# Decoder step on one core: decode masks on another engine, two margins, score order, and reordered first and last steps

## The chip, the cores and the metric

The kernel runs on one core of a Trainium2 chip. The metric is the device time of one execution in microseconds. Engines are named as in the profile: PE is TensorE's matrix multiply and PEld its weight loads, DVE is VectorE, ACT is ScalarE, POOL is GpSimd, SP is SyncE. DMAs are issued from queues on SP, ACT and POOL.

## The reference

One layer of a decoder handles 256 prompt tokens and 8 x 4 decode tokens (288 columns in all), width 2048. It takes an RMS norm and one input projection, then three groups: a short gated convolution (512 channels), sparse attention with 8 query heads in 2 key groups (a compressed, a selected and a window branch), and cross-attention to 256 memory tokens. Each is gated, the three are concatenated, and one output projection, a residual add and a last RMS norm follow.

```python
h = rms_norm(x, norm_g)
c_h, c_b, c_c, c_g, q, n_g, b_g, kv6, m_q, m_g = split_cols(h @ w_in)
...
imp = jnp.where(forced[None, :, None, :], FORCE, imp)
_, idx = lax.top_k(imp, top)                  # 16 blocks of 64 cached keys
s2 = jnp.einsum('bgthd,bgtkjd->bgthkj', qrg, kg) * ATTN_SCALE
p2 = masked_softmax(s2, smask, axis=(-2, -1))
...
return x + mixed @ w_out, kv_new, win_state, conv_new
```

For the decode tokens the selected branch runs over 2048 cached keys per request. The kernel computes the scores of all 2048 and masks the blocks that are not among the chosen ones. The norm needs a reciprocal square root of a mean of squares per token.

## The kernel before

All large products are split in float32r: an operand is taken as a high and a low half (`wh`, `wl` for weights), and three of the four partial products are summed. A weight half tile is 128 x 1024. It is loaded by DMA (`w_load`, from SP at first and from POOL later, five buffers), copied to its high half by ACT (`w_hi`), and the low half is the difference, taken by DVE (`w_lo`). A half tile of the input projection gives 24 matmuls (`product_half`, `run_half`). Everything else is fitted between them.

The order of the work is written by a planner inside the program, at build time. `chunk()` is called after every 12 matmuls and lets each live generator (`spawn`) run to its next `yield`. A list `at` estimates how far PE, the loads, DVE (`VEC`), ACT and SP have come. `until(engine, margin)` yields at least one chunk and goes on only when PE's estimate has passed that engine's estimate plus the margin. The default margin `WAIT` is 0.8; `AHEAD`, -1.5, lets an instruction be placed early. DVE and ACT work issued through `vec` and `act` moves the estimates; work issued straight to POOL (`nc.gpsimd`) does not. Each engine carries out its instructions in the order in which they were written, and waits where data is missing.

What the change touches:

- `first_tiles` (helper of the start): the first two column tiles of the memory projection in float32, from k-tiles that DVE scales as they land (`m_scale`, four k-tiles a call, with a copy of the high half on ACT). `m_low` takes the low half on DVE, `first_loads` issues loads on SP. `part(i, k, n)` issues n k-tiles of column tile i. In the trace these products are `zf`.
- `rsqrt`: called in `token_rstd` (the memory tokens), in `sum_x` (the input tokens) and in `factors` (three times, at the end). One Newton step after it corrects the first value.
- `scores`: scores of four groups of cached keys (512 columns) against the decode queries, in PSUM (`sk`), copied by ACT into a stretch of the wide tile `S`. There is one `S` for each half of the batch (`hf` 0 and 1).
- `dec_cmp`, `dec_softmax`: the compressed branch's importances give `madd`, which is 0 for a chosen block and -1e30 for another. `dec_softmax` adds it to the four stretches of selected scores, takes maxima, exponentials and the scaling, and transposes. It ends by setting a flag that the value products (`winv_use`, `selv_use`, in the trace `od`) wait for.
- `weights`: transposes 512 columns of `S` in four pieces (`pv` in the trace) before each value product.
- `prompt_cmp`, `prompt_nsa`: the prompt's attention. Their transposes are `pct` and `pt`.
- The end: the last 512 output columns come as rows (`zr`), the decode rows from `decode_rows` (`zd`, 16 k-steps of four column groups). `squares`, `factors`, `spread_rows` (`rb`), `scale_rows` and `scale_tiles` do the last norm, each followed by its output DMA. `spread_rows(1, ...)` stands among the decode rows after `SPREAD_AT` k-steps. `busy` fills PE with products that nobody reads.

The decode output is split for the second output pass by `split_decode`; the second pass starts when that has been written.

Of the kernel before, what the change touches and what calls it, by code (L numbers as in the profile page):

```python
# [71 lines left out]
WARM = 3  # L72
LOW_FIRST = 22
TAIL_BUSY = (4, 6)
SPREAD_AT = 13
DT = 12
ROWS = 512

# [2 lines left out]
def decode_step(ctx, tc, xT, xN, xD, xL, fgl, memT, cst, w_in, w_mem, w_out, w_bg, pt, ptv, ckc, ckk, ckv, wk, wv, mk, mv,  # L81
# [112 lines left out]
    def C(name):  # L194
        o, w = _COFF[name]
        return c[:, o:o + w]
# [3 lines left out]
    def rsqrt(r, ssq, rest=None, room=None):  # L200

        v, t = room or (small(3, "yv", 1)[:, :r.shape[1]], small(3, "yt", 1)[:, :r.shape[1]])
        if rest is not None:
            act.activation(r, ssq, AF.Sqrt, scale=1.0 / D, bias=rest[0])
            vec.scalar_tensor_tensor(v, ssq, -0.5 / D, rest[1], op0=ALU.mult, op1=ALU.add)
            vec.reciprocal(r, r)
            vec.scalar_tensor_tensor(t, r, r, v, op0=ALU.mult, op1=ALU.mult)
            vec.scalar_tensor_tensor(r, t, 1.5, r, op0=ALU.add, op1=ALU.mult)
            return
        act.activation(r, ssq, AF.Sqrt, scale=1.0 / D, bias=C("eps"))  # L210
        vec.tensor_scalar(v, ssq, 1.0 / D, EPS, op0=ALU.mult, op1=ALU.add)
        vec.reciprocal(r, r)
        vec.tensor_tensor(t, r, r, op=ALU.mult)
        vec.scalar_tensor_tensor(t, t, -0.5, v, op0=ALU.mult, op1=ALU.mult)
        vec.scalar_tensor_tensor(r, t, 1.5, r, op0=ALU.add, op1=ALU.mult)
# [74 lines left out]
    def first_tiles():  # L290


        z = [pz.tile([128, 512], F32, name=f"zf{i}", tag="z")[:, :256] for i in range(2)]
        def part(i, k, n):
            w = raws[k // 8 * 2 + i]
            for j in range(k, k + n):
                matmul(z[i], w[:, j % 8 * 128:(j % 8 + 1) * 128], m_g(j, 1)[:, 0], start=(j == 0), stop=(j == KT - 1))

        for k0 in (0, 2, 4, 6):
            for i in range(2):  # L300
                part(i, k0, 2)
            if k0 == 2:
                first_loads(0)
                m_scale(8)
                m_low(0)
            elif k0 == 4:
                m_scale(12)
                m_low(4)
            elif k0 == 6:
                for s in range(2):  # L310
                    w_hi(s + 2)
                    w_lo(s + 1)
                    w_load(s + WR)
                first_loads(1)
                for k in (8, 12):
                    m_low(k)
                m_add(4)
                w_hi(4)
                for k in (8, 12):
                    m_square(k)  # L320
            chunk()
        for s in (2, 3):
            w_hi(s + 2)
            w_lo(s + 1)
            part(s - 2, 8, 4)
            chunk()
            part(s - 2, 12, 4)
            w_load(s + WR)
            first_loads(s)
            nhalf[0] = s + 1  # L330
            yield z[s - 2]
# [162 lines left out]
    def scores(hf, o, t, keys):  # L494

        s = pss.tile([128, 512], F32, name=f"sk{hf}", tag="s")
        keys = [keys(x) for x in t]
        for c0 in range(2):
            for g in range(2):
                for b in range(4):  # L500
                    matmul(s[32 * b:32 * b + 32, c0 * 256:c0 * 256 + 256], qcols(0, 4 * hf + b, g), keys[2 * c0 + b // 2](b % 2, g),
                           start=(g == 0), stop=(g == 1), skip_group_check=True)
        act.activation(env["S", hf][:, o:o + 512], s, AF.Copy)


    def selk_load(j, n, t):
# [21 lines left out]
    def wink_use(hf, t):  # L528

        def keys(x):  # L530
            x = x.rearrange("p (b g r) -> p b g r", b=2, g=2)
            return lambda b, g: x[:, b, g, :]

        while "k" not in env:
            yield 1
        scores(hf, C_WIN, t, keys)
        S = env["S", hf]
        s = pss.tile([128, 512], F32, name=f"sn{hf}", tag="s")
        for j in range(2):
            for g in range(2):  # L540
                for b in range(4):
                    matmul(s[32 * b:32 * b + 32, 32 * j:32 + 32 * j], qcols(0, 4 * hf + b, g),
                                     kk[:, 2 * j + g, 256:288], start=(g == 0), stop=(g == 1), skip_group_check=True)
        nmask = C("newmask")[:, hf * 32:(hf + 1) * 32]
        vec.tensor_tensor(S[:, C_NS:C_NS + 32], s[:, 0:32], nmask, op=ALU.add)
        vec.tensor_tensor(S[:, C_NW:C_NW + 32], s[:, 32:64], nmask, op=ALU.add)
        w = S[:, C_NW - 4:C_NW]
        behind(VEC, ACT)
        vec.tensor_tensor(w, w, C("winmask"), op=ALU.add)
        env["keys", hf] = True  # L550
        return
        yield

    def dec_softmax(hf):
# [1 line left out]
            yield 1  # L556
        S = env["S", hf]
        mx = small(8, "mx8", 1)
        for i in range(4):
            sel = S[:, C_SEL + i * 512:C_SEL + (i + 1) * 512].rearrange("p (n j) -> p n j", j=64)  # L560
            vec.tensor_tensor(sel, sel, env["madd", hf][:, i * 8:i * 8 + 8].unsqueeze(2).to_broadcast([128, 8, 64]), op=ALU.add)
            vec.tensor_reduce(mx[:, i:i + 1], sel, axis=AX.XY, op=ALU.max)
            yield 1
        vec.tensor_scalar(S[:, 0:32], S[:, 0:32], gs[:, hf, 0:1], None, op0=ALU.mult)
        vec.tensor_reduce(mx[:, 4:5], S[:, C_NS:C_SEL], axis=AX.X, op=ALU.max)
# [48 lines left out]
    def weights(hf, q):  # L614

        o = C_WIN if q == 0 else C_SEL + (q - 1) * 512
        w = env["S", hf][:, o:o + 512]
        parts = w.rearrange("p (r c) -> p c r", c=4)
        t = ptr.tile([128, 512], F32, name=f"pv{hf}", tag="t")
        for n in range(4):  # L620
            transpose(t[:, n * 128:(n + 1) * 128], parts[:, n, :], ident)
        act.activation(w, t, AF.Copy)
        env["PT", hf, q] = w
# [286 lines left out]

    z0 = zt("C", "zeros")
    nc.gpsimd.memset(z0, 0.0)
    act.activation(small(1, "mx1"), z0[:, 0:1], AF.Sqrt)
    ps = pss.tile([128, 512], F32, name="zeros", tag="s")
    for _ in range(WARM):
        matmul(ps[:, :NT], z0[:, :128], z0, start=True, stop=True)
# [387 lines left out]
    def prompt_cmp():  # L1304
# [47 lines left out]
        for a in range(2):  # L1352
            vec.tensor_tensor(pc3[:, a], pc[:, a].unsqueeze(1).to_broadcast([128, 3, 8, 4]),
                                    smv[:, a].unsqueeze(1).unsqueeze(3).to_broadcast([128, 3, 8, 4]), op=ALU.mult)
        yield from until(VEC)

    def split_values():
        v = xhl.tile([128, 4, 512], F32R, name="v_hl", tag="qk0a")
# [11 lines left out]
    def prompt_nsa(g, tt):  # L1370
# [31 lines left out]
        for br in (1, 2):  # L1402
# [11 lines left out]
            behind(ACT, VEC)  # L1414
            for h in range(4):
                act.activation(P[:, h, :], P[:, h, :], AF.Copy, scale=sm[:, h:h + 1])
            yield from until(ACT)
            PT = []
            for i in range(tt + 1):
                t = ptr.tile([128, 512], F32, name=f"pt{g}{tt}{br}{i}", tag="t")  # L1420
# [184 lines left out]
    def second_pass(n, z):  # L1605
# [8 lines left out]
            vec.tensor_tensor(acc, acc, s, op=ALU.add)  # L1614
        act.activation(y, y, AF.Copy, scale=C("fg")[:, n:n + 1])
        if n == DT - 3:
            act.activation(small(1, "mx1"), C("eps"), AF.Sqrt)

    def first_two():
        s = nhalf[0]  # L1620
# [93 lines left out]
        return r  # L1714

    def spread_rows(g, r):
        n, k = (128, 128) if g < 2 else (32, 32)
        matmul(rb[:, g * 128:g * 128 + n], r[:k].to_broadcast([k, 128]), ident[:k, :n], start=True, stop=True)

    def scale_rows(g, r, eng):  # L1720
        w = part[g].shape[1]
# [55 lines left out]
    busy(TAIL_BUSY[0])  # L1777
    matmul(ssq[:, 3:4], sel, sums2[:, 2:3], start=True, stop=True)
    scale_tiles(1, 4, 8, nc.sync)
    gains(2)  # L1780
    scale_tiles(1, 8, 12, nc.sync)
    r2 = factors(2, ssq[:, 3:4])
    busy(TAIL_BUSY[1])
    spread_rows(2, r2)
# [137 lines left out]
```

## Time and profile before

| | us |
|---|---|
| median of 3 runs (lowest to highest) | 603.91 (602.45 to 604.02) |
| the profiled execution | 602.7 |
| its span, first to last instruction | 600.9 |
| PE busy in the span | 593.2 |
| DVE busy | 457.2 |
| ACT busy | 303.5 |
| POOL busy | 204.3 |
| data moved by DMA | 190.84 MB, 318 GB/s |

The granted clock of TensorE was 0.999. A row of the timeline gives the start, the length, the engine, the line, the operation with what it writes and reads, how many instructions were merged, and in brackets the idle time before the first of them with what ended it. Most instructions of DVE and ACT show line 138, the call inside `Timed`, and most matmuls line 121, since helpers issue them; so the tiles' names tell them apart. Matmuls overlap, so the length of a merged row includes the last one's own length, some 0.3 us. A row for one tile gives shortest, median and longest duration in ns, the first and last start, and the shapes.

### The profile page before, as it was taken

To read this page: it belongs to the slowest core of one execution; us is meant where nothing else is said; L and a number is where in the kernel's file an instruction comes from. 1 tells how busy PE (TensorE), PEld (TensorE's weight loads), DVE (VectorE), ACT (ScalarE), POOL (GpSimd) and SP (SyncE) were. 2 spreads that over 40 slices of the span, in tenths; PEclk is the share of its full clock that TensorE was granted. 3 is DMA by queue.
4 is the path that set the end of the run, shared out by engine and by line. 5 is a ranking of instruction groups with operands and counts; after the bars stand their busy time and mean duration, and the time that the engine had idled before them with its cause. 6 is when DMAs were issued, how large, how long until landed. Compare 5 with 4: busy or idle time off the path is not lost.

```text
span 600.9 us, 13265 instructions
## 1 busy us (share of the span) xinstructions
PE 593.2 (99%) x4827; PEld 544.4 (91%) x4827; DVE 457.2 (76%) x739; ACT 303.5 (51%) x541; POOL 204.3 (34%) x281
## 2 busy tenths in 40 slices
PE   8999999999999999999999999999999999999997
PEld 6987999989999999989999899999998998979996
DVE  3999799988596679978897879887768742357665
ACT  4887446444456434434455444555553453435653
POOL 2013554434245333414554544223111334422200
PEclk9999999999999999999999999999999999999999
DMA  8999888999989998987799898898989999979834
GB/s 306 416 429 399 272 306 319 325 306 375 326 269 370 380 415 308 342 327 248 265 331 326 286 368 289 276 339 290 317 311 331 363 333 318 326 253 365 280 143 159
DMA packets 76194, 190.84 MB, mean 318 GB/s; under 512 B 8864, under 2 KB 26432, under 8 KB 75872
## 3 DMA queue, kind: packets, MB, share of 16 engines
q0 software_dynamic: 26016, 100.48, 47.4%
q1 hardware_dynamic: 49104, 88.12, 40.8%
q10 hardware_dynamic: 1008, 1.38, 0.7%
q8 instruction: 38, 0.62, 0.4%
q14 instruction: 28, 0.23, 0.1%
HBM read 184.74 MB, written 13.60 MB: 330 GB/s over the span
## 4 chain that ended last, share of the span: by engine, by line
PE 87%; DVE 7%; DMA 3%; issue 1%; ACT 1%; ACTq 0%; SPq 0%; DVEq 0%
PE z L121 61%; PE zr L121 4%; PE zv L121 4%; PE od L121 3%; PE sk L121 3%; DMA mraw<-memT 2%; DVE pooled L138 2%; PE s L121 2%; DVE wl L138 2%; PE acc L121 2%; PE pv L126 1%; PE pt L126 1%; PE zf L121 1%; DMA st<-ckc 1%; PE om L121 1%
## 5 line engine op out<-in xcount | busy, mean ns | idle before, releaser
L121 PE MATMUL z<-x,wh 128*128 128x288 f32 x1664 | 248.2, 298 | 0.4 <-ACT wh L138 0.4
L121 PEld LDWEIGHTS z<-x,wh 128*128 128x128 f32 x1664 | 227.4, 188 | 7.0 <-issue 4.2
L138 DVE TENSOR_TENSOR wl<-w,wh 128x1024 fp32r<-128x1024 f32 x147 | 181.7, 1239 | 63.7 <-PE z L121 33.2
L138 ACT ACTIVATE wh<-w 128x1024 fp32r<-128x1024 f32 x148 | 154.3, 1052 | 20.0 <-PE z L121 13.1
L121 PE MATMUL z<-x,wl 128*128 128x288 f32 x832 | 127.0, 295 | 0.6 <-DVE wl L138 0.6
L121 PEld LDWEIGHTS z<-x,wl 128*128 128x128 f32 x832 | 115.3, 188 | 1.5 <-DVE wl L138 1.4
L415 POOL TENSOR_TENSOR st<-st,cst 128x512 f32<-128x512 f32 x56 | 62.3, 1112 | 109.5 <-issue 55.5
L230 POOL DMA_DIRECT2D w<-w_in x104 | 58.4, 562 | 111.9 <-DVE wl L138 79.3
L138 DVE TENSOR_REDUCE pooled<-st 128x16 f32<-128x1024 f32 x56 | 67.7, 1210 | 2.2 <-POOL st L415 2.1
L138 DVE TENSOR_TENSOR st<-st,cst 128x512 f32<-128x512 f32 x56 | 39.1, 697 | 8.0 <-DMA st<-ckc 7.9
L230 POOL DMA_DIRECT2D w<-w_out x32 | 17.6, 551 | 67.3 <-DVE wl L138 42.1
L642 POOL DMA_INDIRECT st<-ckv,rows_v x29 | 31.5, 1087 | 22.0 <-PE od L121 13.0
L138 ACT ACTIVATE P<-P,nm 128x128 f32<-128x128 f32 (+1 forms) x32 | 14.2, 444 | 30.3 <-DVE nm L138 30.3
L121 PE MATMUL z<-y,wh 128*128 128x288 f32 x192 | 27.2, 294 | 0.0
L121 PEld LDWEIGHTS z<-y,wh 128*128 128x128 f32 x192 | 26.0, 188 | 0.1
L121 PE MATMUL sk<-st,qz 128*32 128x256 f32 x288 | 19.7, 382 | 0.0
L121 PE MATMUL od<-st,S 128*32 128x256 f32 x288 | 18.9, 382 | 0.0
L138 ACT ACTIVATE se<-z 128x288 f32<-128x288 f32 x16 | 6.4, 401 | 22.0 <-PE z L121 22.0
L121 PE MATMUL zf<-mixed,w 128*128 128x256 f32 x64 | 15.3, 394 | 1.0 <-DVE mixed L138 0.7
L121 PEld LDWEIGHTS zf<-mixed,w 128*128 128x128 f32 x64 | 12.0, 194 | 4.7 <-DVE mixed L138 2.4
L121 PE MATMUL z<-y1b,wh 128*128 128x288 f32 x84 | 15.3, 296 | 0.0
L138 ACT ACTIVATE P<-P,sm 128x128 f32<-128x128 f32 (+1 forms) x32 | 11.9, 444 | 6.4 <-DVE sm L138 6.2
(356 smaller groups left out, 813.2 us busy)
## 6 DMA issues: line engine op xcount, KB each, us to landing
w<-w_in POOLq DMA_DIRECT2D x104, 512.0 KB, 6.3
st<-ckc SPq DMA_DIRECT2D x112, 256.0 KB, 5.9
w<-w_out POOLq DMA_DIRECT2D x32, 512.0 KB, 6.2
st<-ckk SPq DMA_DIRECT2D x112, 128.0 KB, 4.9
w<-w_mem SPq DMA_DIRECT2D x12, 512.0 KB, 7.4
o_wk<-wk POOLq DMA_DIRECT2D x8, 512.0 KB, 7.5
o_wv<-wv POOLq DMA_DIRECT2D x8, 512.0 KB, 7.3
qk<-ckc SPq DMA_DIRECT2D x16, 256.0 KB, 6.2
```

The costliest lines, as they stand in the source:

```text
L121: nc.tensor.matmul(out, a, b, **kw)
L126: nc.tensor.transpose(out, a, b)
L138: return getattr(self.engine, name)(*args, **kw)
L230: (nc.gpsimd if s >= ON_SYNC else nc.sync).dma_start(raws[s], wsrc[s])
L415: done.append(eng.tensor_tensor(tm[:, :, kv], tm[:, :, kv], acmp[:, kv].unsqueeze(1).unsqueeze(1).to_broadcast([128, 2, 4, 64]), op=ALU.mu ...
L642: nc.gpsimd.indirect_dma_start(t, None, ckv, bass.IndirectOffsetOnAxis(ap=rows_v[:, j * 4 + b:j * 4 + b + 1], axis=0))
```

## The change

- `first_tiles`: k-tiles 8 to 11 of both column tiles are issued before k-tiles 12 to 15 of either. `m_low(0)` goes in front of `m_scale(8)`, `m_low(4)` in front of `m_scale(12)`. The number of chunks stays.
- `rsqrt`: ACT computes the reciprocal square root itself, and DVE's reciprocal is left out.
- `scores` writes each stretch of `S` so that the 128 columns of one transpose lie side by side; ACT reads PSUM with a step of four for that. `weights` reads them in sequence. The window mask then lies on four columns 128 apart.
- `dec_softmax`: POOL adds the mask, DVE takes the maximum one yield later. There is one yield more than before.
- Margins: the end of `prompt_cmp` waits for DVE's estimate plus 1.8 instead of 0.8, `prompt_nsa` for ACT's plus 1.2 instead of 0.8.
- The end: `SPREAD_AT` is 11 instead of 13, `spread_rows` uses 128 rows for the decode tokens too, and one `scale_tiles` (with its output DMA on SP) moves in front of `gains(2)`.

```diff
-SPREAD_AT = 13
+SPREAD_AT = 11
...
-            act.activation(r, ssq, AF.Sqrt, scale=1.0 / D, bias=rest[0])
+            act.activation(r, ssq, AF.Abs_reciprocal_sqrt, scale=1.0 / D, bias=rest[0])
             vec.scalar_tensor_tensor(v, ssq, -0.5 / D, rest[1], op0=ALU.mult, op1=ALU.add)
-            vec.reciprocal(r, r)
...
-        act.activation(r, ssq, AF.Sqrt, scale=1.0 / D, bias=C("eps"))
+        act.activation(r, ssq, AF.Abs_reciprocal_sqrt, scale=1.0 / D, bias=C("eps"))
         vec.tensor_scalar(v, ssq, 1.0 / D, EPS, op0=ALU.mult, op1=ALU.add)
-        vec.reciprocal(r, r)
...
-        for k0 in (0, 2, 4, 6):
+        for k0 in (0, 2, 4, 6, 8, 10):
             for i in range(2):
                 part(i, k0, 2)
             if k0 == 2:
+                m_low(0)
+                m_scale(8)
                 first_loads(0)
-                m_scale(8)
-                m_low(0)
             elif k0 == 4:
+                m_low(4)
                 m_scale(12)
-                m_low(4)
...
-            part(s - 2, 8, 4)
-            chunk()
             part(s - 2, 12, 4)
...
-        act.activation(env["S", hf][:, o:o + 512], s, AF.Copy)
+        act.activation(env["S", hf][:, o:o + 512].rearrange("p (c r) -> p c r", c=4), s.rearrange("p (r c) -> p c r", c=4), AF.Copy)
...
-        w = S[:, C_NW - 4:C_NW]
+        w = S[:, C_WIN:C_NW].rearrange("p (c r) -> p c r", c=4)[:, :, 127]
...
-        for i in range(4):
-            sel = S[:, C_SEL + i * 512:C_SEL + (i + 1) * 512].rearrange("p (n j) -> p n j", j=64)
-            vec.tensor_tensor(sel, sel, env["madd", hf][:, i * 8:i * 8 + 8].unsqueeze(2).to_broadcast([128, 8, 64]), op=ALU.add)
-            vec.tensor_reduce(mx[:, i:i + 1], sel, axis=AX.XY, op=ALU.max)
+        for i in range(5):
+            if i < 4:
+                sel = S[:, C_SEL + i * 512:C_SEL + (i + 1) * 512].rearrange("p (c n j) -> p c n j", c=4, j=16)
+                madd = env["madd", hf][:, i * 8:i * 8 + 8].unsqueeze(1).unsqueeze(3).to_broadcast([128, 4, 8, 16])
+                nc.gpsimd.tensor_tensor(sel, sel, madd, op=ALU.add)
+            if i > 0:
+                vec.tensor_reduce(mx[:, i - 1:i], S[:, C_SEL + (i - 1) * 512:C_SEL + i * 512], axis=AX.X, op=ALU.max)
             yield 1
...
-        parts = w.rearrange("p (r c) -> p c r", c=4)
+        parts = w.rearrange("p (c r) -> p c r", c=4)
...
-    act.activation(small(1, "mx1"), z0[:, 0:1], AF.Sqrt)
+    unit = small(1, "mx1")
+    nc.gpsimd.memset(unit, 1.0)
+    act.activation(unit, unit, AF.Abs_reciprocal_sqrt)
...
-        yield from until(VEC)
+        yield from until(VEC, WAIT + 1.0)
...
-            yield from until(ACT)
+            yield from until(ACT, WAIT + 0.4)
...
-            act.activation(small(1, "mx1"), C("eps"), AF.Sqrt)
+            act.activation(small(1, "mx1"), C("eps"), AF.Abs_reciprocal_sqrt)
...
-        n, k = (128, 128) if g < 2 else (32, 32)
-        matmul(rb[:, g * 128:g * 128 + n], r[:k].to_broadcast([k, 128]), ident[:k, :n], start=True, stop=True)
+        n = 128 if g < 2 else 32
+        matmul(rb[:, g * 128:g * 128 + n], r.to_broadcast([128, 128]), ident[:, :n], start=True, stop=True)
...
+    scale_tiles(1, 8, 12, nc.sync)
     gains(2)
-    scale_tiles(1, 8, 12, nc.sync)
```

## The prediction

> **What bounds the kernel now.** I read the page's busy line first, then the sums by stage, then TensorE's own waits, and last the timeline at each wait, which the parts below quote.
>
> ```profile
> PE 593.2 (99%) x4827; PEld 544.4 (91%) x4827; DVE 457.2 (76%) x739; ACT 303.5 (51%) x541; POOL 204.3 (34%) x281
> 0.00:20.00 20.00, 17.89 (x68) 13.56 (x69) 10.06 (x21) 10.42 (x12) 3.77 (x13) 1.00 0.91 334
> 228.00:268.00 40.00, 39.18 (x331) 35.57 (x330) 35.90 (x72) 17.94 (x28) 11.38 (x18) 1.00 0.90 323
> ```
>
> TensorE (PE) has a matmul in flight for 593.2 of 600.9 us, and the change removes no matmul. So almost nothing can be won by making another engine faster: only PE's few waits, the spacing of its own instructions, and the two ends are for sale. The stage rows (stage, length, then busy time of PE, weight load, DVE, ACT, POOL) give the places: the first 20 us lack 2.1 us of PE, the stretch 228 to 268 lacks 0.8; the rest of the idle time lies in single waits and behind the last matmul. Each part of the change goes to one of these, so I price them one by one. The profiled execution took 602.7 us, its span and 1.8 us around it. It lies 1.2 us under the median of the runs, 603.91; I take the sum off the profiled time and carry the difference over to the median.
>
> **Start: the order of the first tiles.** Now k-tiles 8 to 15 of the first column tile come before those of the second; after, 8 to 11 of both come before 12 to 15 of either.
>
> ```profile
> 10.36 4.58 PE L121 MATMUL zf<-mixed,w 128*128 128x256 f32 x20 [0.25 <-DMA w<-w_mem]
> 15.24 5.45 PE L121 MATMUL zf<-mixed,w 128*128 128x256 f32 x24 [0.29 <-DVE mixed L138]
> 11.00 0.62 DVE L138 TENSOR_SCALAR mixed<-mraw,mraw 128x256 f32<-128x256 f32 x2 [1.66 <-DMA mraw<-memT]
> 7.47 0.33 SPq L230 DMA_DIRECT2D w<-w_mem  x1
> w<-w_mem SPq DMA_DIRECT2D x1, 512.0 KB, 6.7
> 20.35 0.81 PE L121 MATMUL z<-m0a,wh 128*128 128x256 f32 x4
> 21.82 0.28 PE L121 MATMUL z<-m0a,wh 128*128 128x256 f32 x1
> 20.86 1.22 DVE L138 TENSOR_TENSOR wl<-w,wh 128x1024 fp32r<-128x1024 f32 x1
> 22.13 0.39 PE L121 MATMUL z<-m0a,wl 128*128 128x256 f32 x1
> ```
>
> PE stops between the two zf blocks until DVE has scaled k-tile 12. A matmul leaves two records; 20 records in 4.58 us, the last about 0.38 long and the first 0.10 late, are 0.216 apart. In the new order records 17 to 20 of the first block read the fourth weight tile, issued at 7.47 and landed 6.7 us later, at 14.17. PE is there at 10.36 + 0.10 + 16 x 0.216 = 13.92. It then waits for that weight instead, and the remaining 28 records end the block at 14.17 + 0.10 + 6.05 = 20.32, against z's start at 20.35 now. So the wait changes its name: nothing gained if the tile is as late as here, 0.38 (20.35 - 19.97) if it is early. The first low-half subtraction (1.22, the shape of the wl at 20.86) moves into the 1.66 us that DVE idles before 11.00, the second takes its old place, which puts the chain to the first wl (20.86) some 1.2 us earlier, and the first product's third term, at 22.13 instead of some 0.12 after its neighbour at 21.82, no longer stops: 0.19. ScalarE's and SP's own orders stay, since only DVE work changes place beside the loads. Taken: **-0.2**, bounds -0.6 and +0.1 (a weight tile a little later).
>
> **Reciprocal root in one step.**
>
> ```profile
> L138 ACT ACT_TABLE_LOAD x3 | 3.8, 1283 | 4.6 <-DMA w<-w_mem 4.6
> 596.11 0.15 DVE L138 RECIPROCAL yr<-yr 128x1 f32<-128x1 f32 x1
> ```
>
> Each of five calls loses a DVE reciprocal of 0.15 us or so. Two lie under the first products, where PE never waits for them (0). The trace shows no such function. It shows that Copy and Square ran beside Sqrt without a table load, so I take no more loads than the present three. If each change between it and Copy or Square needed one, the last 10 us would pay 1283 ns several times. From below, nothing but the reciprocals can be gained.
>
> **Scores in transposed order.** Ten times four transposes (pv) read S with a step of four floats, afterwards in sequence.
>
> ```profile
> L126 PE MATMUL pv<-cst,S x40: 281/285/388, 251.3 to 520.5; 128*128 128x128 f32 x40
> L126 PE MATMUL pt<-cst,P x48: 270/272/328, 288.4 to 423.8; 128*128 128x128 f32 x48
> L138 ACT ACTIVATE S<-sk x10: 597/598/600, 133.1 to 453.1; 128x512 f32<-128x512 f32 x10
> ```
>
> The same instruction on sequential data takes 272 ns instead of 285. PE is full there, so 40 x 13 ns = **-0.5**, bounds -0.6 and 0. The step goes into ScalarE's copy out of PSUM (598 ns), of which no strided row exists. It is hidden while ScalarE is half idle: even doubled, the ten copies are 6 us on an engine with 297 us free. Its lower bound is no gain.
> [...]
>
> **Masking on GpSimd.**
>
> ```profile
> L138 DVE TENSOR_TENSOR S<-S,madd x8: 679/684/685, 225.5 to 464.0; 128x512 f32<-128x512 f32 x8
> L415 POOL TENSOR_TENSOR st<-st,cst x56: 1082/1092/1601, 58.2 to 428.0; 128x512 f32<-128x512 f32 x56
> 234.20 0.53 POOL L230 DMA_DIRECT2D w<-w_in  x1 [3.56 <-DVE wl L138]
> 235.50 2.27 PE L121 MATMUL z<-x,wh 128*128 128x288 f32 x16
> 237.06 2.35 DVE L138 TENSOR_TENSOR wl<-w,wh 128x1024 fp32r<-128x1024 f32 x2
> 238.33 1.33 PE L121 MATMUL z<-x,wl 128*128 128x288 f32 x8 [0.56 <-DVE wl L138]
> 239.50 1.75 PE L121 MATMUL z<-x,wh 128*128 128x288 f32 x12
> 240.16 1.15 POOL L415 TENSOR_TENSOR st<-st,cst 128x512 f32<-128x512 f32 x1 [1.06 <-DVE st L138]
> 240.72 1.67 DVE L138 TENSOR_TENSOR wl<-w,wh 128x1024 fp32r<-128x1024 f32 x1
> ```
>
> In the first softmax DVE lags PE by several us and PE stops at 238.33 for wl. The half from 235.50 to 239.50 takes 4.00 us; 24 matmuls at 1.58 us per 12 take 3.16. The stall's whole price is 0.84. Four masks of 0.68 leave DVE, 2.7 us. GpSimd needs 1.09 to 1.60 us for this shape (the nearest row, the cached keys' product). Its queue also holds weight issues that wait for DVE's wl (234.20), so I follow both queues from 225.5. GpSimd finishes the product before the masks at 226.9, mask 0 at 228.0 and, behind two DMA issues, mask 1 at 230.3, mask 2 at 231.4. DVE's maximum over piece i comes one step after mask i; DVE stands before the first at about 227.5 and before the second at 228.8, so it waits 0.5 and 1.5 us; the third and fourth are ready. DVE reaches the wl that PE lacked at about 235.7 instead of 237.06, done by 236.9. PE wants it at 235.50 + 2.11 = 237.6. There is 0.7 us to spare; a wl that runs beside a GpSimd product (240.72, with 240.16) takes 1.67 instead of 1.22, and one or two such may eat most of it. Taken **-0.7**, bounds -0.84 and +0.7 (DVE later by what two waits of 1.7 us cost beyond the 2.7 us saved). Behind a waiting GpSimd mask stand weight loads: 0.5 us of issue each, needed four half tiles (12.6 us) later. The second softmax has no PE wait to remove. Its chain grows by one step, which is taken up under the rivals.
>
> **The two margins.**
>
> ```profile
> 265.50 1.74 PE L121 MATMUL z<-x,wh 128*128 128x288 f32 x12
> 267.50 0.28 PE L126 MATMUL pct<-cst,pc 128*96 128x128 f32 x1 [0.26 <-DVE pc L138]
> 269.20 0.56 PE L121 MATMUL z<-x,wh 128*128 128x288 f32 x3
> 345.63 0.66 PE L126 MATMUL pt<-cst,P 128*128 128x128 f32 x4 [0.25 <-ACT S L138]
> 366.62 0.93 PE L126 MATMUL pt<-cst,P 128*128 128x128 f32 x4
> ```
>
> The longer margins make the writer of PE's order put further matmuls in front of these transposes. The half at 265.50 takes 3.70 us against 3.16 plus 0.11 for the transpose: 0.43 lost. Of that 0.26 is the idle time shown, 0.17 lost overlap. The group at 345.63 idles 0.25 and loses, at the same rate, about 0.42. The group at 366.62 takes 0.93 instead of the 0.66 of its like: 0.27. Together 1.12. The second one waits for a PSUM copy behind pv rather than for its own data, so the margin removes it only by moving it; and each move shifts the prompt chain by 12 matmuls, which may land another piece badly. Taken **-0.8**, bounds -1.2 and +0.3 (about one new stall of these sizes).
>
> **Tail.**
>
> ```profile
> 592.28 1.28 PE L121 MATMUL zd<-w,mixed 128*32 128x128 f32 x40
> 593.49 0.49 PE L121 MATMUL rb<-cst,yr 128*128 128x128 f32 x2
> 594.01 1.28 DVE L138 TENSOR_TENSOR yo<-ysum,rb 128x512 f32<-128x512 f32 x2 [1.14 <-PE rb L121]
> 595.68 0.26 ACT L138 ACTIVATE yr<-ssqy,yrest 128x1 f32<-128x1 f32 x1 [0.47 <-PE ssqy L121]
> 596.29 0.22 DVE L138 SCALAR_TENSOR_TENSOR yt<-yr,yv 128x1 f32<-128x1 f32 x1
> ```
>
> rb moves forward by two of the sixteen decode k-steps. Each holds 8 records in four column groups, 0.22 us by the rows between 592.28 and rb (40 records, five steps, in 1.21 us less one restart), so 0.44. DVE's scalings start at 593.57, all three are done before 595.7 and no longer stand in front of the last row factor. That factor then follows ScalarE's result (595.94) directly, at 595.97 instead of 596.29: **-0.3** to the last output DMA. The moved output DMA goes to an SP queue that is idle then. The 128-row spread instead of 32 is a like matmul (0). Bounds -0.4 and 0.
>
> **Sum:** -0.2 - 0.5 - 0.7 - 0.8 - 0.3 = -2.5, less 0.4 for one fresh stall somewhere, the size of those just listed: -2.1. From the profiled execution 602.7 - 2.1 = 600.6; from the median **601.8**.
>
> **Rivals.** *Stalls move and do not go.* New margins and a shorter DVE queue reshuffle everything after 225 us; four old stalls become others. Only the spacing of pv and the tail remain, 0.8: 603.1. For it: three separate stalls of 0.3 to 0.8 arose from coincidences. Against: DVE does get emptier.
>
> *Contention keeps the wl stall.* If masks and wl hold each other (240.72: +0.45 each), DVE gains little and the 0.7 is gone: 602.5. For it: both orders are close together at 225 to 237. Against: maxima stand between them.
> [...]
>
> *Slower: the decode output comes late for the second pass.*
>
> ```profile
> 487.48 2.73 PE od L121 x36
> 529.92 1.86 PE od L121 x32
> 536.92 0.42 DVE L138 TENSOR_TENSOR y<-mixed,y 128x256 fp32r<-128x256 f32 x1 [0.49 <-ACT y L138]
> 540.31 2.27 PE L121 MATMUL z<-y,wh 128*128 128x288 f32 x16
> ```
>
> The second softmax gets one step more. Its five value products follow each other by loads, 487.48 to 529.92, so a late first one delays all. The last one's split ends at 537.34, PE needs it at 540.31: 3.0 us of slack. One step (1.6 us) fits. From 3 us on PE idles. At a slip of 8 us (three steps, where two of the places lie 24 matmuls apart) it idles 5: 601.8 + 5 = 606.8. Against: the shorter DVE estimate gives part of the step back.
>
> **How the numbers follow.** Forecast 601.8 with 0.55 (its own range 600.4 to 602.9), moved stalls 0.25, contention 0.10, late decode 0.10. All low bounds together (-3.6) give 600.3; 600.2 to 604.4 leaves out the late decode and a little more. I call 0.3% (1.8 us) what can be told from no change. Faster: 0.43 of the first, 0.03 and 0.02 of the next two, 0.48. Slower: the late decode, 0.10. Same: 0.42.
>
> **What would show it.** zf without the stop at 15.24 but with one for w near 14; pv at about 272 ns; no wait of z for wl near 238, and DVE maxima that wait for POOL S; pct and pt without waits; the last output DMA issued 0.3 us earlier from the last decode matmul. I am wrong if PE waits in new places for over 1 us together, if table loads appear in the tail, or if PE idles before the second pass.

## The result, and the profile after

The changed kernel takes 607.91 us (median; 606.42 to 608.11 for all executions but one disturbed one) against 603.81 us before on the same chip: **1.0066 times as long, 95% interval 1.0052 to 1.0081**. That is 4.0 us slower, where 2.1 us faster was forecast. The profiled execution took 606.42 us with a span of 604.7, 3.7 us more than before.

First the page's busy line of the changed kernel, then what PE waited for. A row of waits gives what waited for what, the total in us, how many times, and the longest in us.

```profile
PE 594.0 (98%) x4827; PEld 545.2 (90%) x4827; DVE 459.6 (76%) x726; ACT 302.9 (50%) x541; POOL 220.4 (36%) x290
```

DVE has 13 instructions fewer than before (eight masks and five reciprocals), and yet its busy time rose by 2.4 us. What PE waited for:

```profile
PE z L121 <- DVE wl L138: 1.7, 2, 1.3
PE kcT L121 <- DVE PT L138: 1.3, 1, 1.3
...
PE acc L121 <- DVE pcT L138: 0.7, 2, 0.5
...
PE ot L126 <- DVE odr L138: 0.4, 1, 0.4
...
PE z L121 <- ACT y1b L138: 0.2, 1, 0.2
PE z L121 <- DVE se L138: 0.2, 1, 0.2
```

The waits for pct and pt are gone; the experiments show which part removed them. In their place stand kcT 1.3, acc 0.7, ot 0.4, y1b and se 0.2 each. The wl wait did not go: 0.6 has become 1.7 in two stops. All these lie between 230 and 485 us (left out are waits at the start and the wh wait of before); the matmul that stands at 134 us starts 0.2 us earlier than before, the one at 513 us 4.1 later. The timeline around the first softmax shows the wl stops:

```profile
226.10 1.66 DVE L138 TENSOR_TENSOR wl<-w,wh 128x1024 fp32r<-128x1024 f32 x1
226.65 2.03 POOL L559 TENSOR_TENSOR S<-S,madd 128x512 f32<-128x512 f32 x1
...
228.72 0.69 DVE L138 TENSOR_REDUCE mx<-S 128x1 f32<-128x512 f32 x1 [0.95 <-POOL S L559]
...
229.32 1.10 DVE L138 TENSOR_TENSOR st<-st,cst 128x512 f32<-128x512 f32 x1
...
232.06 2.79 DVE L138 TENSOR_TENSOR wl<-w,wh 128x1024 fp32r<-128x1024 f32 x1
232.15 2.27 PE L121 MATMUL z<-x,wh 128*128 128x288 f32 x16
232.36 1.05 POOL L559 TENSOR_TENSOR S<-S,madd 128x512 f32<-128x512 f32 x1
...
233.95 1.81 POOL L559 TENSOR_TENSOR S<-S,madd 128x512 f32<-128x512 f32 x1
...
234.91 1.31 PE L121 MATMUL z<-x,wl 128*128 128x288 f32 x8 [0.49 <-DVE wl L138]
235.80 0.69 DVE L138 TENSOR_REDUCE mx<-S 128x1 f32<-128x512 f32 x1 [0.35 <-POOL S L559]
...
236.06 2.27 PE L121 MATMUL z<-x,wh 128*128 128x288 f32 x16
...
236.41 1.21 DVE L138 TENSOR_REDUCE pooled<-st 128x16 f32<-128x1024 f32 x1
...
238.32 1.22 DVE L138 TENSOR_TENSOR wl<-w,wh 128x1024 fp32r<-128x1024 f32 x1
...
239.59 1.32 PE L121 MATMUL z<-x,wl 128*128 128x288 f32 x8 [1.25 <-DVE wl L138]
...
240.75 1.48 PE L121 MATMUL z<-x,wh 128*128 128x288 f32 x10
```

Two masks beside one wl stretch it from 1.22 to 2.79 us. Of the masks that meet a wl one takes 1.05 us, the others 1.81 and 2.03; by what the two lengthen each other no run shows. (The wl at 226.10 has another POOL product beside it too, and takes 1.66 also in a kernel below with no mask on POOL.) The half tiles from 232.15 and 236.06 take 3.91 and 4.69 us; against 3.16 that is 0.75 + 1.53 = 2.28 lost, where 0.84 was lost before.

Further on, a stop that did not exist before:

```profile
439.52 1.04 PE L126 MATMUL pt<-cst,P 128*128 128x128 f32 x8
...
441.12 1.29 DVE L138 TENSOR_TENSOR PT<-pt,PT 128x512 fp32r<-128x512 f32 x2 [0.20 <-ACT PT L138]
...
441.87 0.70 PE L121 MATMUL kcT<-pooled,cst 128*128 128x256 f32 x2 [1.31 <-DVE PT L138]
```

Two pt blocks fill both tiles of the PSUM pair `ptr`. kcT, next in PE's list, wants a tile of that pair and waits until DVE has read the first.

### The profile page after: what moved, and what is told of

The parts are those of the page before. It is cut to its first block, busy times and chain, and to the rows that moved or that the text cites. A ratio compares the mean times of both kernels' runs of the same rounds, so it can differ in the third digit from the quotient of the medians.

```text
span 604.7 us, 13264 instructions
## 1 busy us (share of the span) xinstructions
PE 594.0 (98%) x4827; PEld 545.2 (90%) x4827; DVE 459.6 (76%) x726; ACT 302.9 (50%) x541; POOL 220.4 (36%) x290
## 4 chain that ended last, share of the span: by engine, by line
PE 54%; DVE 5%; issue 1%; ACT 1%; POOL 1%; DVEq 0%; ACTq 0%
PE z L121 37%; PE zr L121 4%; PE od L121 3%; PE acc L121 2%; PE s L121 2%; PE sk L121 2%; DVE wl L138 1%; PE pv L126 1%; PE pt L126 1%; PE zd L121 1%; PE omd L121 1%; PE smd L121 1%; POOL S L559 1%; DVE pcT L138 1%; DVE pooled L138 1%
## 5 line engine op out<-in xcount | busy, mean ns | idle before, releaser
L138 DVE TENSOR_TENSOR wl<-w,wh 128x1024 fp32r<-128x1024 f32 x147 | 186.4, 1271 | 62.5 <-PE z L121 26.1
L411 POOL TENSOR_TENSOR st<-st,cst 128x512 f32<-128x512 f32 x52 | 58.8, 1132 | 81.9 <-DVE st L138 36.4
L138 DVE TENSOR_REDUCE pooled<-st 128x16 f32<-128x1024 f32 x52 | 62.9, 1210 | 2.1 <-POOL st L411 2.1
L641 POOL DMA_INDIRECT st<-ckv,rows_v x29 | 35.4, 1220 | 26.8 <-PE od L121 16.5
L138 DVE TENSOR_TENSOR st<-st,cst 128x512 f32<-128x512 f32 x52 | 36.0, 691 | 8.9 <-DMA st<-ckc 8.6
L411 POOL TENSOR_TENSOR qk<-qk,cst 128x512 f32<-128x512 f32 x12 | 14.6, 1213 | 38.4 <-DVE qk L138 24.4
L138 ACT ACTIVATE S<-sk 128x512 f32<-128x512 f32 x10 | 6.0, 597 | 22.2 <-PE sk L121 22.2
L121 PEld LDWEIGHTS zf<-mixed,w 128*128 128x128 f32 x64 | 13.5, 213 | 3.7 <-DVE mixed L138 1.6
```

The source lines that it names most:

```text
L121: nc.tensor.matmul(out, a, b, **kw)
L138: return getattr(self.engine, name)(*args, **kw)
L411: done.append(eng.tensor_tensor(tm[:, :, kv], tm[:, :, kv], acmp[:, kv].unsqueeze(1).unsqueeze(1).to_broadcast([128, 2, 4, 64]), op=ALU.mu ...
L641: nc.gpsimd.indirect_dma_start(t, None, ckv, bass.IndirectOffsetOnAxis(ap=rows_v[:, j * 4 + b:j * 4 + b + 1], axis=0))
```

## The experiments

The list in which PE gets its instructions is written at build time, so it can be compared between kernels without timing: for each piece (pt, pct, acc, od, sk, ...) I count the product matmuls that stand ahead of it. That is called PE's order below; the other engines' lists are written along with it. All twelve kernels of this section ran beside the kernel before, in three batches on three chips. Each ratio is to the kernel before in the same batch, and kernels are compared by these ratios.

| masks on | PE's order written as if masks took | margins | ratio | 95% interval |
|---|---|---|---|---|
| DVE | DVE time | old | 0.9989 | 0.9973 to 1.0005 |
| DVE | DVE time | both long | 0.9984 | 0.9969 to 0.9999 |
| POOL | DVE time | both long | 0.9979 | 0.9967 to 0.9990 |
| POOL | nothing | old | 0.9983 | 0.9972 to 0.9994 |
| POOL | nothing | pct long | 1.0006 | 0.9993 to 1.0019 |
| POOL | nothing | pt long | 1.0037 | 1.0022 to 1.0052 |
| POOL | nothing | both long (the change) | 1.0066 | 1.0052 to 1.0081 |
| DVE | nothing | both long | 1.0050 | 1.0032 to 1.0068 |

(All eight have the new start, root, tail and score order. The rows written for "nothing" also have the softmax's extra step, those written for "DVE time" do not.)

**One part taken back or done alone.** First the changed kernel with the masks on DVE again, and without the softmax's extra step (the one yield more):

```diff
-                nc.gpsimd.tensor_tensor(sel, sel, madd, op=ALU.add)
+            vec.tensor_tensor(sel, sel, madd, op=ALU.add)
+            vec.tensor_reduce(mx[:, i:i + 1], S[:, C_SEL + i * 512:C_SEL + (i + 1) * 512], axis=AX.X, op=ALU.max)
```

> The changed kernel with the four masks of each softmax back on DVE (in the new score order); everything else as changed. Three theories of the 4.1 us lost. MASKS: the adds on GpSimd carry the loss, by the two wl stalls (0.65 and 1.41 us of lost PE time at 234.9 and 239.6 in the changed kernel, against 0.72 at 238.3 before) and by the order of PE that they set free; then this kernel keeps only the gains of the other parts and comes to 602.4 to 603.4 us, with no wl stall above 0.8 and no wait at kcT. MARGINS: the longer margins moved pt against kcT (1.13 us lost at 441.9) and acc against pcT (0.36 and 0.19 at 316.8 and 279.0); then those 1.7 us stay, only the wl stalls shrink by 1.3, and the time is about 606.5. ENDS: start and tail carry it; then 606.5 to 608 with the PE offset at 25 us already above 1.

Measured: 602.14 us, 0.9984 (0.9969 to 0.9999). The loss is gone, and of PE's waits behind 200 us these are all that is left:

```profile
PE z L121 <- DVE wl L138: 0.6, 1, 0.6
...
PE pt L126 <- ACT S L138: 0.2, 1, 0.2
```

This fits MASKS, and speaks against ENDS and against MARGINS as it stood (606.5).

Then the mask alone with its extra step, in the kernel before:

```diff
-            vec.tensor_tensor(sel, sel, env["madd", hf]...
+                nc.gpsimd.tensor_tensor(sel, sel, env["madd", hf]...
```

> The kernel before with the masks on GpSimd alone (scores in their old order, old margins, old ends). MASKS: 606 to 608.5 us, the wl stalls near 235 to 240 add up to about 2 us, further stalls follow between 250 and 470. MARGINS: 603.8 + 1.3 for the wl stalls = 605.1 at the most, kcT without a wait. ENDS: 603.8 + 1.3 or less.

Measured: 603.64 us, 1.0008 (0.9998 to 1.0018). MASKS is refuted as it stood: alone, the masks cost 0.5 us by the ratio, 1.1 at the most. PE's waits show why it is so little (left out are those at the start, and two that the kernel before has too: wh 0.4 and rb 0.2):

```profile
PE z L121 <- DVE wl L138: 1.7, 2, 1.2
```

The wl wait is the changed kernel's 1.7, but pct and pt are no longer in the list, although the margins are the old ones. Moving the masks had already moved those pieces by 12 or 24 matmuls in PE's order. Together their stops were priced at 1.1 us, which would pay most of the wl stops back. The longer margins then had nothing left to remove.

The changed kernel with the old margins:

```diff
-        yield from until(VEC, WAIT + 1.0)
+        yield from until(VEC)
...
-            yield from until(ACT, WAIT + 0.4)
+            yield from until(ACT)
```

> The changed kernel with the two margins back at their default, masks still on GpSimd. MASKS: 606.5 to 608.5 us, within 1 us of the changed kernel's 607.9. MARGINS: kcT and acc lose their waits, 607.9 - 1.7 = 606.2, and pct (0.43) and pt (0.42, 0.27) stall again: 607.3 or less. A time under 605 would say that margins and masks together did it.

Measured: 601.86 us, 0.9983 (0.9972 to 0.9994). So neither part costs the 4 us by itself: it takes masks and margins together. Its PE waits have no kcT, acc or ot among them; behind 130 us this is the only row:

```profile
PE z L121 <- DVE wl L138: 1.8, 2, 1.3
```

The sums by stage (stage, length, busy us of PE, weight load, DVE, ACT, POOL) say the same. Changed kernel first, then the one with the old margins:

```profile
264.00:404.00 140.00, 138.88 (x1129) 129.70 (x1128) 119.95 (x191) 67.76 (x143) 64.45 (x73) 1.00 0.88 308
404.00:470.00 66.00, 64.69 (x600) 58.09 (x599) 46.98 (x88) 31.95 (x65) 17.99 (x22) 1.00 0.88 297
```

```profile
264.00:404.00 140.00, 140.00 (x1156) 130.27 (x1156) 122.70 (x196) 70.48 (x155) 60.80 (x73) 1.00 0.89 311
404.00:470.00 66.00, 66.00 (x601) 61.23 (x601) 47.38 (x92) 32.47 (x60) 18.79 (x25) 1.00 0.89 312
```

With the old margins PE is never idle from 264 to 470 us; with the long ones it idles 1.12 + 1.31 us (two acc and ot, then kcT). Over the same product matmuls, from the one at 134 us to the one that stands at 513 us in the kernel before, the two differ by 4.4 us (383.2 against 378.8). Five waits (kcT, two acc, ot, y1b) are 2.6 of it; five restarts at the prediction's 0.17 would be another 0.9, an estimate. The remaining 0.9 I have not traced further than to more changes between kinds of matmul. The wait for se is not counted here: it also appears below with the old margins (early masks on DVE), and it is missing in the kernel below with masks on DVE in the changed kernel's order, which has the long ones.

The ends alone (start, root, tail):

```diff
-SPREAD_AT = 13
+SPREAD_AT = 11
...
-            act.activation(r, ssq, AF.Sqrt, scale=1.0 / D, bias=rest[0])
+            act.activation(r, ssq, AF.Abs_reciprocal_sqrt, scale=1.0 / D, bias=rest[0])
...
-        for k0 in (0, 2, 4, 6):
+        for k0 in (0, 2, 4, 6, 8, 10):
```

> The kernel before with only the start, the one-step reciprocal root and the tail changed. MASKS and MARGINS: 603.1 to 603.8 us (the tail gives 0.13 us by the profile from the last row sums to the last output, 2.46 against 2.33; the start 0 to 0.4). ENDS: 605 or more.

Measured: 602.65 us, 0.9990 (0.9976 to 1.0004). ENDS falls. A gain of 0.6 us is the best estimate, and no gain at all is not excluded.

**Order or engine?** Moving the masks changes PE's order: the planner counts DVE's work and not POOL's, and the softmax has one step more. It also changes which engine does the adds. Two kernels separate order and engine. In the first, POOL does the masks, but the planner is told that DVE does, and the extra step is taken out:

```diff
                 nc.gpsimd.tensor_tensor(sel, sel, madd, op=ALU.add)
+                at[VEC] = max(at[VEC], at[0]) + 2 * (0.03 + 0.0011 * 512)
             if i > 0:
-                vec.tensor_reduce(...)
-            yield 1
+                nc.vector.tensor_reduce(...)
+            if i < 4:
+                yield 1
```

> The changed kernel, masks on GpSimd, but the writer of PE's order is told that they take DVE's time (0.59 us each), and the last maximum no longer takes a step of its own: PE's order is that of the kernel with DVE masks (602.1 us), matmul for matmul, while the masks run on GpSimd. ORDER (the loss is in the place of pieces in PE's order, which the masks and the margins set together): 602.1 plus at most 1.4 for the wl stalls near 240, so 602 to 603.5 us. ENGINE (the loss comes from GpSimd and DVE holding each other, or from DVE waiting for GpSimd): 605.5 to 608.

Measured: 602.42 us, 0.9979 (0.9967 to 0.9990). In the second, the mirror, DVE does the masks, but the planner isn't told, and the extra step stays:

```diff
-                nc.gpsimd.tensor_tensor(sel, sel, madd, op=ALU.add)
+                nc.vector.tensor_tensor(sel, sel, madd, op=ALU.add)
```

> The mirror: masks on DVE, but not told to the writer of PE's order, so that PE's order is that of the changed kernel (607.9 us), matmul for matmul. ORDER: 605.5 to 608 us, with the waits of kcT, acc and the second pass as in the changed kernel. ENGINE: 602 to 603.5.

Measured: 606.33 us, 1.0050 (1.0032 to 1.0068). These are its first waits:

```profile
PE z L121 <- DVE wl L138: 1.4, 1, 1.4
PE kcT L121 <- DVE PT L138: 1.3, 1, 1.3
```

ORDER holds in both directions: POOL masks with DVE's order are fast, DVE masks with POOL's order are slow and stop at kcT just so. In the table, the order is worth 0.0066 (DVE masks) to 0.0087 (POOL masks) of the time, 4.0 to 5.2 us; POOL instead of DVE makes -0.0005 in the one order and +0.0016 in the other, with overlapping intervals. The wl wait is 1.4 us even with DVE's masks, so most of its growth belongs to the order.

The first of the two kernels undoes two things at once, the missing count and the extra step, and no run separates them. The planner's lists do, for two kernels that were written out but not timed. With the extra step alone, or the missing count alone, the long margins move no piece by more than 36 matmuls, and kcT stands 12 or 60 matmuls from the nearest pt instead of in the same gap. So the order of the changed kernel takes all three: uncounted masks, the extra step and the longer margins.

**Which margin?** Each one alone, with the masks on POOL and not counted. Without pt's:

```diff
-            yield from until(ACT, WAIT + 0.4)
+            yield from until(ACT)
```

> The changed kernel without the longer margin of pt (ScalarE's), with that of pct (DVE's). Its PE order differs in one pct from the kernel with both margins back (601.9 us). ORDER, with the loss from pt's margin: 601.5 to 602.5 us. If the loss hung on pct's margin: 605 or more.

Without pct's:

```diff
-        yield from until(VEC, WAIT + 1.0)
+        yield from until(VEC)
```

> The changed kernel without the longer margin of pct, with that of pt. Its PE order differs in one pct from the changed kernel's. ORDER, with the loss from pt's margin: 606.5 to 608.5 us. If the loss hung on pct's margin: 603 or less.

Measured: 604.07 us, 1.0006 (0.9993 to 1.0019), and 605.87 us, 1.0037 (1.0022 to 1.0052). Both expectations were too simple: from 0.9983 without either, pct's margin costs 0.0023 (1.4 us, though the intervals just touch) and pt's 0.0054 (3.3 us), and together they make 0.0083. The lists say how. pct's margin moves one pct by 12 matmuls in PE's list and nothing else there; but DVE's list changes with it in two places. Near 279 us pcT's low half now stands behind a wl, 0.21 us late. At the second, the changed kernel has

```profile
314.27 0.68 DVE L138 TENSOR_TENSOR qk<-qk,cst 128x512 f32<-128x512 f32 x1
...
315.04 1.09 POOL L411 TENSOR_TENSOR qk<-qk,cst 128x512 f32<-128x512 f32 x1 [3.18 <-DVE qk L138]
...
315.31 1.37 DVE L138 TENSOR_TENSOR pcT<-pcT,cst 96x512 fp32r<-96x512 f32 x1
...
316.82 0.47 PE L121 MATMUL acc<-pcT,vcp 96*128 96x512 f32 x1 [0.52 <-DVE pcT L138]
```

and the kernel with the old margins

```profile
313.30 0.69 DVE L138 TENSOR_TENSOR pcT<-pcT,cst 96x512 fp32r<-96x512 f32 x1
313.91 0.68 DVE L138 TENSOR_TENSOR qk<-qk,cst 128x512 f32<-128x512 f32 x1
...
314.74 0.40 PE L121 MATMUL acc<-pcT,vcp 96*128 96x512 f32 x1
```

The product qk of the cached keys has moved in front of pcT. It costs its own 0.68, and it sets off its POOL twin, beside which pcT takes 1.37 instead of 0.69. So acc, right in time before, waits 0.52. Between the kernels without and with pct's margin the stretch from 134 us on grows by 1.16 us in the traces, and the two acc stops with what follows them on PE are all of it.

pt's margin moves one pt by 12 matmuls near 340 us, the next pieces by 36, 48, 60, and those near 400 us by 108 (4.5 half tiles), since each piece of the prompt's chain is placed after the one before it and at whole steps of 12. So pt and kcT, 72 matmuls apart with the old margins, come to stand in the same gap. With the masks counted, the same two margins move pieces by 24 at most, in no such way, and cost nothing that can be measured (0.9989 against 0.9984).

**The kcT stop itself.** The changed kernel, with kcT in a PSUM tile of the other pair, in unchanged order:

```diff
-        t = ptr.tile([128, 512], F32, name=f"kcT{hf}", tag="t")
+        t = pss.tile([128, 512], F32, name=f"kcT{hf}", tag="s")
```

> The changed kernel, where kcT's product takes a PSUM tile of the scores' pair instead of one of the pair that pt's transposes use; PE's order is unchanged. BUFFER (kcT stops at 441.9 because both tiles of the pair still hold pt until DVE has taken the low part of PT): the stall of 1.13 us goes, and 607.9 becomes 606.4 to 606.9 us. If kcT waits for its own data (pooled), the stall stays and so does 607.9.

Measured: 606.18 us, 1.0050 (1.0035 to 1.0066). Its timeline at that place:

```profile
440.03 1.04 PE L126 MATMUL pt<-cst,P 128*128 128x128 f32 x8
...
440.90 0.60 PE L121 MATMUL kcT<-pooled,cst 128*128 128x256 f32 x2
```

kcT follows pt at once, without its stop: BUFFER. The gain in time, 0.0016 (1.0 us), fits the 1.1 expected, but the intervals overlap, so the row is the proof here and not the time. This profiled execution also has a wait that the changed kernel's hasn't: imp, 1.12 us at 212.62, behind DVE work that waited 3.37 us for a DMA of cached keys. So the spans of the two executions can't be compared.

**The score order alone,** on top of the ends:

```diff
-        act.activation(env["S", hf][:, o:o + 512], s, AF.Copy)
+        act.activation(env["S", hf][:, o:o + 512].rearrange("p (c r) -> p c r", c=4), s.rearrange("p (r c) -> p c r", c=4), AF.Copy)
...
-        parts = w.rearrange("p (r c) -> p c r", c=4)
+        parts = w.rearrange("p (c r) -> p c r", c=4)
```

> Start, reciprocal root, tail and the new score order, with the masks on DVE and the old margins; PE's order is that of the kernel before but for rb. What the score order gives alone: pv at about 272 ns against 285, 0.5 us under the 602.65 of the ends alone, so 602.1 us. The kernel with the two margins on top (602.1) then says what the margins do while the masks are counted: nothing if this one is within 0.5 of it, a gain if this one is at 602.8 or more (pct's 0.42 and a pt gone), a loss if it is at 601.5 or less. If the strided copy of the scores (597 ns as before) or the layout cost something, 602.7 or more with pv still at 285.

Measured: 603.41 us, 0.9989 (0.9973 to 1.0005), the same ratio as the ends alone (0.9990). The 602.1 expected was missed, and the time is inconclusive for 0.5 us; the rows are clear. Here are pv's weight loads before, then loads and matmuls now, then the copy of the scores in the changed kernel:

```profile
L126 PEld LDWEIGHTS pv<-cst,S x40: 195/212/224, 251.1 to 520.4; 128*128 128x128 f32 x40
```

```profile
L126 PEld LDWEIGHTS pv<-cst,S x40: 137/140/143, 252.5 to 521.6; 128*128 128x128 f32 x40
L126 PE MATMUL pv<-cst,S x40: 270/272/331, 252.6 to 521.7; 128*128 128x128 f32 x40
```

```profile
L138 ACT ACTIVATE S<-sk x10: 597/597/598, 133.0 to 456.8; 128x512 f32<-128x512 f32 x10
```

At its place the order gives more than forecast. From the start of the matmul in front of each group of four pv to the start of the first one behind it, the ten groups take 7.63 us in the kernel with the ends alone and 6.80 us here, 0.82 less. The profiled execution hands that back: imp waits 0.98 us at 213.60 behind DVE work, as in the profile above, where DVE had waited 3.37 us for a DMA of cached keys, and some 0.6 us go among the scores near 452 to 455, where the cause is not traced.

The two margins on top of this kernel change nothing measurable (0.9984 against 0.9989). The expectation's rule, in microseconds, would have read 603.41 against 602.14 as a gain; but the two ran on different chips, and the ratios don't show it.

**A version that beats both.** The masks need only `madd` (216.9 us) and the four stretches of scores, all there 8 us before the window's scores. So they can be issued at once, in the changed kernel with the old margins; the maxima stay where they were:

```diff
     def dec_softmax(hf):
+        while not all(env.get(("sk", hf, i)) for i in range(4)):
+            yield 1
+        ... (the four masks, nc.gpsimd.tensor_tensor)
         while not env.get(("keys", hf)):
             yield 1
...
         scores(hf, C_SEL + pp * 512, t, keys)
+        env["sk", hf, pp] = True
```

> The changed kernel with the old margins (601.9 us), and the four masks issued to GpSimd as soon as madd exists (216.9 in the kernel before) instead of one per step behind the window's scores (from 225); PE's order is that of the 601.9 kernel, matmul for matmul. PLACE (the two wl stalls of 0.66 and 1.41 us come from DVE waiting for masks and from masks beside wl): both go or shrink under 0.4 in all, and the time is 600.0 to 600.8 us. If they come from DVE's own load in this stretch, they stay and the time is 601.5 to 602.3.

and the same with the masks on DVE (`nc.vector`, not counted):

> The early masks on DVE instead of GpSimd, with PE's order again that of the 601.9 kernel. If only the place counts: within 0.5 us of the kernel with early masks on GpSimd, as DVE has its 2.7 us of masks behind it before 225. If DVE is short of time there too: a wl stall of 0.5 to 1.5 us appears between 217 and 240 and the time is 0.6 to 1.6 us above it.

Measured: 600.60 us, **0.9953 (0.9935 to 0.9971)**, on POOL, and 600.66 us, **0.9955 (0.9942 to 0.9969)**, on DVE. PLACE: with PE's order untouched, both beat the 0.9983 of late masks by 0.0028 to 0.0030 (1.7 to 1.8 us), somewhat under the 2.28 us that the two wl stops took. The profile with early masks on POOL, first its timeline and then the sum over the stretch:

```profile
218.42 6.31 POOL L559 TENSOR_TENSOR S<-S,madd 128x512 f32<-128x512 f32 x4 [1.48 <-DVE madd L138]
220.17 1.63 DVE L138 TENSOR_TENSOR wl<-w,wh 128x1024 fp32r<-128x1024 f32 x1
222.05 1.76 DVE L138 TENSOR_TENSOR wl<-w,wh 128x1024 fp32r<-128x1024 f32 x1 [0.25 <-issue]
```

```profile
224.00:244.00 20.00, 20.00 (x215) 18.36 (x208) 17.48 (x31) 9.63 (x14) 9.25 (x14) 1.00 0.94 359
```

The masks still slow two wl (1.63 and 1.76), but where DVE has slack; PE has no idle time from 224 to 244. Both versions are also faster than the kernel before, by 3.0 and 2.9 us. Between the engines no difference can be measured.

## Why the prediction was wrong, point by point

**The two margins** (taken -0.8, bounds -1.2 and +0.3): the step that failed. It said that "each move shifts the prompt chain by 12 matmuls, which may land another piece badly", and bounded that by one stall of the sizes seen. Wrong twice. The shift is not 12 but grows along the chain to 108, and it made five new stops instead of one. On the masks' order the margins cost 0.0083 of the time, 5.0 us. The old stops of pct and pt, 1.12 together, are gone indeed, but moving the masks had already removed them. The prediction priced each part against the kernel before and added; these two act through one list of estimates and don't add.

**GpSimd masks** (taken -0.7, bounds -0.84 and +0.7): wrong in sign. Two DVE waits for masks came, 0.95 us before the first maximum and 0.35 before the fourth, where 0.5 and 1.5 before the first two were forecast. Mis-sized was the price of a wl beside POOL: 0.45 more was allowed for each of one or two; two masks beside one wl cost 1.57 (1.22 to 2.79). And a term was missing: DVE's list was taken to stay as it was but for the masks. In the changed kernel cached-key work stands in front of the wl at 238.32, the add of 1.10 at 229.32 and the sum of 1.21 at 236.41. In the kernel before, the same add came behind the late wl, and the same sum at 244.24:

```profile
239.33 0.69 DVE L138 TENSOR_TENSOR st<-st,cst 128x512 f32<-128x512 f32 x1
```

The mirror kernel has the new list with masks on DVE, and PE waits 1.40 us for that wl. With the old list it waits 0.56 with masks on DVE and 0.96 with masks on POOL, and in the changed kernel 1.74. So of the 1.2 us by which the idle time grew, about 0.8 came with the list and 0.3 to 0.4 with the engine. DVE ended the wl that PE needs at 239.5, where 236.9 was forecast and 237.6 allowed. The stage went from 0.84 to 2.28 lost, +1.44, past the upper bound. In total the masks alone cost next to nothing (1.0008), which fits the moved pct and pt giving about 1 us back.

**Rivals.** "Stalls move and do not go" was the right picture at the wrong price: it kept the balance at zero, and a list that PE must follow in order has no such balance. "Contention keeps the wl stall" was right that the stall would stay; it expected no change there and got a doubled one, and the contention is the smaller part of that. That masks and wl hold each other up is what the rows show: 2.79 us for a wl against 1.22, and 1.81 and 2.03 for a mask against 1.05. Which of the two is held is not told by which began first: the wl began at 232.06, and yet the mask of 232.36 ran in its 1.05. "The decode output comes late" did not happen: no wait stands before the second pass.

**Score order** (-0.5): pv fell from 285 to 272 ns as forecast, and the weight loads from 212 to 140. The term was too small: at their places the ten groups take 0.82 us less, because the four matmuls of a group also follow each other more closely (the row of a group is 0.64 to 0.75 us long before, 0.60 to 0.66 in the changed kernel), which the sum of 40 x 13 ns left out. The time of the whole kernel shows neither figure; both are below what the intervals tell. Reading PSUM with a step of four cost ACT nothing: 598 ns before, 597 after. The doubling that the prediction allowed for did not come.

**Start, root and tail** (-0.2, 0, -0.3): the ends alone give 0.9990, 0.6 us, against 0.5 forecast, with no change inside the interval. At the start the stop at 15.24 and the one before the first product's third term (22.13) are gone in the changed kernel, as forecast. A stop for a weight tile between 14.2 and 15.8 us came in four of the twelve profiled executions with the new start. Their first z begins anywhere from 19.88 to 21.94 us, so a single profile can't show 0.2 us there. The table loads stayed at three:

```profile
L138 ACT ACT_TABLE_LOAD x3 | 3.8, 1283 | 4.9 <-DMA w<-w_mem 4.8
```

The last output DMA follows the last row sums by 2.33 us instead of 2.46, 0.13 gained and not 0.3. The prediction let the factor's second DVE step (yt) start right behind ACT's result; but the first one (yv) waits for that result too, as the bracket of its row says, and comes in between. The two ends of it before, and then in the changed kernel:

```profile
595.32 0.32 PE L121 MATMUL ssqy<-ysums,both 128*128 128x1 f32 x2
...
597.78 0.33 SPq L1731 DMA_DIRECT2D o_y<-yod  x1
```

```profile
599.27 0.31 PE L121 MATMUL ssqy<-ysums,both 128*128 128x1 f32 x2
...
599.61 0.26 ACT L138 ACTIVATE yr<-ssqy,yrest 128x1 f32<-128x1 f32 x1 [0.47 <-PE ssqy L121]
599.91 0.16 DVE L138 SCALAR_TENSOR_TENSOR yv<-ssqy,yrest 128x1 f32<-128x1 f32 x1 [0.31 <-ACT yr L138]
...
601.60 0.33 SPq L1732 DMA_DIRECT2D o_y<-yod  x1
```

**The range** (600.2 to 604.4) missed because no case had several new stalls from one shift. Even all the upper bounds together (+0.1, +0.7 and +0.3) with the fresh stall of 0.4 give 605.4 from the median, against 607.91 measured. The prediction's own sign of failure, waits in new places for over 1 us together, did appear.

## What to carry to other kernels

Where a planner writes a fixed order from estimates, moving work to an engine that it doesn't count, adding a step, or lengthening a margin is a change of that order: compare the two instruction lists first, and follow each moved piece to the buffers and engines that its new neighbours use. Parts that act through the same estimates are priced together, not one by one and added. An engine that is given work to relieve another should get it as early as its data allow: the early place was worth 1.8 us here, the choice of the engine nothing that could be measured.

## What the runs showed of the hardware that was not expected

- A DVE subtraction of 128x1024 (1.22 us alone) took 2.79 us beside two POOL adds of 128x512, and such an add up to 2.03 instead of 1.05. Four masks less saved DVE 2.7 us; the one stretched wl (1.57) and the two waits for masks (0.95 and 0.35) took 2.9 back.
- The step of four floats is paid by the transposes' weight loads (212 against 140 ns) more than by their matmuls (285 against 272), and by ACT's read of PSUM not at all (597 ns).
